# Ten slots instead of eight for the activation channel tiles of the in-projections

## The chip, the cores and the metric

The kernel runs on one core of one Trainium2 chip. The metric is the device time of one launch in microseconds, as the median of several runs. TensorE (PE) multiplies, VectorE (DVE), ScalarE (ACT) and GpSimd (POOL) do the elementwise work, and SyncE (SP) issues nearly all DMAs. Each engine, and SP's queue, works through its instructions in order: one that waits holds all behind it.

## The reference

One decoder layer of width 1024 on 2048 tokens, in float32. A normalized input goes through one combined projection, which feeds two groups of heads; both results meet in one output projection, and an MLP follows:

```python
u = rms_norm(h, norm_pre_mix[i])
q, k, v, qi, ki, wi, z, xbc, dt = jnp.split(u @ w_in[i], offsets, axis=-1)
ki = layer_norm(ki, k_idx_ln_w[i], k_idx_ln_b[i])
attn = sparse_attention(q, k, v, qi, ki, wi, rel_bias)   # each query keeps its best 256 keys
ssd = ssd_mixer(z, xbc, dt, ...)                         # convolution, chunked state scan, gate
h = h + rms_norm(jnp.concatenate([attn, ssd], -1) @ w_out[i], norm_post_mix[i])
f = jnp.square(jax.nn.relu(rms_norm(h, norm_pre_mlp[i]) @ w_mlp_up[i])) @ w_mlp_down[i]
h = h + rms_norm(f, norm_post_mlp[i])
```

The indexer's score of query t and key s is a sum over four small heads, `w[t,h] * relu(qi[t,h] . ki[s])`; the 256 largest scores of a query among the keys up to t take part in its softmax, with a bias by distance.

## The kernel before, in words

**Products.** A float32 operand is held as two parts, a rounded main part ("hi") and the rest ("lo"), and each product is three matmuls that add up in one PSUM bank: hi·hi (L257), hi·lo (L260), lo·hi (L261). Weights come by DMA into a raw tile (`load_w`, L246, tile `wr`) and are split by GpSimd into `wh` (L231) and `wl` (L232).

**The in-projections.** The tokens are cut into four tiles of 512. For each, `in_proj(t)` makes 20 products with the same eight activation channel tiles `u` (128 channels by 512 tokens, hi beside lo): first one of 76 columns with the weights `w_misc` (the index keys, the index weights and the time steps), then eight for the convolution inputs, two of index queries, four of gates, one of keys, one of values, and four of queries. Every product goes through the channels k = 0 to 7 in order, three matmuls each, 24 in all.

**The activation tiles.** `moving(t)` makes them. For each channel it takes a slot of the ring `u` and one of the ring `wr` (four slots, shared with all raw weights), loads the raw channel by DMA (`xr`, L301), writes hi on ScalarE (L311) and lo on VectorE (L312); for channels 3, 5 and 7 ScalarE scales the raw tile (L305) and copies hi (L308), and GpSimd makes lo (L309). `moving(t + 1)` stands at the last query product of tile t. Ring `u` has eight slots, so channel k of the next tile takes the slot of channel k of this one, and is written after that channel's last three matmuls. Below, the passage from the last product of a tile to the 76-column product of the next is called a change of tile; there are three.

**What runs beside them.** The main sequence is woven with other tasks by due times: the state scan of the SSM heads (`ssd`, with the tiles `si`, `cb`, `lm`, `xd`, the products `p_y`, `p_st`), the top-k search (`topk`: scores `p_ix` into rows `sc`, then counts by sign on ScalarE, `junk_k`, L610), and attention (`attention`: scores `p_s` from query stacks `qs`, bias rows `tq`, softmax rows `pp`, transposes `p_pt`, copies `ppt`, sums `p_o`, result `atp`). Queries pass through DRAM: ScalarE and GpSimd make `qp`, a DMA stores it to `q_d` (L393), and four small DMAs per block load `qs` (L570). Each task has a priority, and a scheduler of the framework puts all instructions of an engine into one order by its own model of times. The orders shown below are the result.

**Behind them.** The pool `front` is closed, and four windows follow, one per token tile: the output projection (`out_proj`: eight `mix` tiles, which take slots of the same ring `u`, L770; sums, and per block of tokens the residual `xh`, L801), and the MLP, whose activations (`u2`) take `u` slots too. Rest of the top-k and attention tasks is woven into the first three.

**Rings.** A tile is taken by `tl(tag, ...)` (L74 on), which asks `place(tag)` for a pool, a number of slots and a name. Where `rings` has an entry for the tag, `place` goes round that list; else the pool goes round its own slots.

Of the kernel before, what the change touches and what calls it, by code (L numbers as in the profile page):

```python
# [41 lines left out]
def hybrid_layer(ctx, tc, x, x_t, w_cols, n_post_mix, n_post_mlp, w_in, w_misc, dt_bias, a_log, d_skip,  # L42
# [11 lines left out]
    FC, BC = (2,3)  # L54
# [4 lines left out]
    WR = 4  # L59
    COMMON = dict(u=8, wr=WR, wl=WL, wh=WL, rsb=1, sc=2, mkk=1, qi=1, ks=2)  # L60
    ATT = dict(c2=2, qs=2)
    FRONT = dict(c4=FC, x24=1, m4=2, m2=3, kc=2, tq=1, mk=1)
    BACK = dict(c4=BC, x8=2, g4=9, m2=2)
    SSD = dict(si=3, cb=2, lm=1, xd=1)
    SIDE = [dict(kc=3, tq=1, mk=1), dict(kc=2, tq=1)]
# [1 line left out]
    where = {}  # L67
# [5 lines left out]
    rings = {}  # L73
# [12 lines left out]
    def phase(name, sizes, smalls=None, side="left"):  # L86
        stack = ExitStack()
        pool = stack.enter_context(tc.tile_pool(name=name, bufs=1, side=side, reuse_waits="tile"))
        use(pool, sizes)
        if smalls:  # L90
            use(pool, {smalls: 2})
        return stack
# [13 lines left out]
    def banks(name, sizes):  # L106
        stack = ExitStack()
        use(stack.enter_context(tc.tile_pool(name=name, bufs=1, space=PSUM, reuse_waits="tile")), sizes)
        return stack

    def const(ap, shape, name, dt=F32):
        t = cp.tile(shape, dt, name=name)
        SP.dma_start(t, ap)
        return t
# [6 lines left out]
    scan = phase("scan", SSD, "ssm", "right")  # L121
    front = phase("front", FRONT, "s")
    side_banks = banks("bank0", BANKS[0])
    NF = 4
    where["row"] = max(1024, 2 * NF * P)
    cols = const(w_cols, [P, 62], "cols")
    ident = const(c_ident, [P, P], "ident")
    junk_k = cp.tile([P, L], I8, name="junk_k")
# [805 lines left out]
    def weave(main, tasks):  # L934

        left = [[*e, 0] for e in tasks]
        now = 0.0
        while True:
            w = step("m", main)
            if w is None:  # L940
                break
            now += w
            for e in left:
                kind, g, n, a, b, done = e
                want = n * min(max((now - a) / (b - a), 0.0), 1.0)
                while e[5] < want:
                    e[5] += 1
                    step(kind, g)
                if now >= b and done <= n:
                    e[5] = n + 1  # L950
                    for _ in g:
                        pass
        for e in left:
            for _ in e[1]:
                pass

    def chain(*gens):
        for g in gens:
            yield from g
# [27 lines left out]
        tasks.append(ctask(range(4, NF), *PF))  # L987
    weave(chain(*(in_proj(t) for t in range(NT))), tasks)
    front.close()
    state["win"] = "1"  # L990
    back = ctx.enter_context(phase("back", BACK, "s"))
    MB = 4
# [95 lines left out]
```

## Time and profile before

| | |
|---|---|
| runs | 2916.97, 2921.40, 2927.34 us, median 2921.4 |
| the profiled execution | 2928.29 us |
| its span | 2926.5 us |
| TensorE busy | 2761.9 us, 94% of the span |
| GpSimd, VectorE, ScalarE busy | 60%, 56%, 51% |
| DMA | 383.46 MB, 131 GB/s on average |
| mean granted clock of TensorE | 0.973 of full |

The profile is that of one execution. A row of a timeline gives the start in us, the duration, the engine and line, the operation, the tile written and those read, the count, and, in brackets, how long the engine idled before it and what ended that. In the table by stretches a pair such as 19.99 (x107) is busy time and instructions of an engine, PEclk is the granted clock as a share of full speed, and the DMA share is the mean busy share of the sixteen DMA engines. The durations of matmuls overlap, since they are pipelined; the starts tell the pace.

### The profile page before, as it was taken

The numbers are of one execution on the slowest core, as the hardware profiler recorded it, in microseconds if no ns is written. First come the engines' busy times: TensorE is split into PE (matmuls) and PEld (weight loads), VectorE is DVE, ScalarE is ACT, GpSimd is POOL, SyncE is SP. The second block draws the span as 40 slices with busy tenths as digits, with TensorE's granted clock in tenths as the row PEclk, the third lists the DMA queues.
The fourth block names the chain that finished last, engine by engine and source line by source line (L and its number), as shares of the span: only waits on it lengthen the run. The fifth ranks groups of instructions, "written<-read, shape, count | busy, mean of one in ns | idle before, by whom it ended". The sixth has DMA issues, their size and how long they took to land.

```text
span 2926.5 us, 41201 instructions
## 1 busy us (share of the span) xinstructions
PE 2761.9 (94%) x13558; PEld 2250.7 (77%) x13558; DVE 1642.4 (56%) x4106; ACT 1481.5 (51%) x2550; POOL 1762.6 (60%) x1721
## 2 busy tenths in 40 slices
PE   7988989789989999998999999999999999999998
PEld 5766767667768887887787888878888888778886
DVE  5479588888575666747765565666444342511113
ACT  2375477675837575677773847644332332311101
POOL 4666556667666656654456575644564656588775
PEclk8999989999989999999999999999999999999999
DMA  3765654634733333255223222553222225522222
GB/s 128 224 189 151 218 157 149 208 118 160 249 120 119 112 103 102 90 176 180 101 94 98 90 97 79 170 177 102 87 95 81 93 78 177 204 95 97 95 94 86
DMA packets 286741, 383.46 MB, mean 131 GB/s; under 512 B 26520, under 2 KB 151360, under 8 KB 286528
## 3 DMA queue, kind: packets, MB, share of 16 engines
q1 hardware_dynamic: 286528, 380.84, 40.0%
q8 instruction: 107, 1.75, 0.2%
q14 instruction: 106, 0.87, 0.1%
HBM read 316.44 MB, written 64.30 MB: 130 GB/s over the span
## 4 chain that ended last, share of the span: by engine, by line
PE 67%; DVE 13%; ACT 6%; DMA 5%; issue 4%; POOL 3%; SPq 1%; POOLq 0%; DVEq 0%; ACTq 0%
PE p_mm L257 9%; PE p_mm L261 9%; PE p_mm L260 9%; PE p_dn L260 7%; PE p_dn L261 7%; PE p_dn L257 7%; ACT junk_k L610 5%; PE p_o L725 4%; PE p_s L683 4%; PE p_pt L717 3%; POOL wl L232 2%; PE p_ix L591 1%; DVE cnd L618 1%; PE p_acc L260 1%; PE p_acc L257 1%
## 5 line engine op out<-in xcount | busy, mean ns | idle before, releaser
L232 POOL TENSOR_TENSOR wl<-wr,wh 128x512 fp32r<-128x512 f32 (+1 forms) x740 | 987.0, 1335 | 179.6 <-ACT wh L229 107.0
L231 POOL TENSOR_SCALAR wh<-wr 128x512 fp32r<-128x512 f32 x674 | 449.6, 667 | 752.1 <-PE p_mm L260 372.8
L257 PE MATMUL p_mm<-u,wh 128*128 128x512 f32 (+1 forms) x1696 | 685.4, 404 | 47.4 <-ACT u L311 15.4
L261 PE MATMUL p_mm<-u,wl 128*128 128x512 f32 (+1 forms) x1696 | 682.8, 404 | 13.2 <-POOL wl L232 12.9
L260 PE MATMUL p_mm<-u,wh 128*128 128x512 f32 (+1 forms) x1696 | 674.9, 398 | 0.6 <-POOL u L309 0.3
L610 ACT ACTIVATE junk_k<-sc,cnd 128x512 int8<-128x512 f32 (+10 forms) x434 | 576.4, 1328 | 157.8 <-DVE cnd L618 122.2
L257 PEld LDWEIGHTS p_mm<-u,wh 128*128 128x128 f32 (+1 forms) x1696 | 322.9, 190 | 119.3 <-ACT u L311 17.5
L260 PE MATMUL p_dn<-wl,g 128*128 128x512 f32 x1008 | 402.2, 399 | 4.2 <-POOL wl L232 4.2
L261 PE MATMUL p_dn<-wh,g 128*128 128x512 f32 x1008 | 399.5, 397 | 2.7 <-POOL g L836 2.7
L261 PEld LDWEIGHTS p_mm<-u,wl 128*128 128x128 f32 (+1 forms) x1696 | 322.5, 190 | 88.7 <-POOL wl L232 21.3
L260 PEld LDWEIGHTS p_mm<-u,wh 128*128 128x128 f32 (+1 forms) x1696 | 322.6, 190 | 69.6 <-DVE u L312 2.3
L257 PE MATMUL p_dn<-wh,g 128*128 128x512 f32 x1008 | 328.0, 398 | 1.9 <-POOL wh L231 1.3
L834 ACT ACTIVATE r<-r 128x512 f32<-128x512 f32 x128 | 80.4, 629 | 437.1 <-DVE r L833 436.7
L688 DVE CUSTOM_DVE_ANT_0 pp<-p_s,mk 128x512 f32<-128x512 f32 (+3 forms) x320 | 192.5, 607 | 134.3 <-PE p_s L683 130.5
L719 ACT ACTIVATE ppt<-p_pt 128x512 fp32r<-128x512 f32 (+1 forms) x288 | 155.3, 568 | 208.1 <-PE p_pt L717 170.0
L720 DVE TENSOR_TENSOR ppt<-p_pt,ppt 128x512 fp32r<-128x512 f32 (+1 forms) x288 | 182.6, 655 | 129.6 <-ACT ppt L719 126.9
L260 PEld LDWEIGHTS p_dn<-wl,g 128*128 128x128 f32 x1008 | 190.3, 189 | 46.8 <-POOL wl L232 5.5
L261 PEld LDWEIGHTS p_dn<-wh,g 128*128 128x128 f32 x1008 | 190.3, 189 | 43.8 <-POOL g L836 3.1
L257 PEld LDWEIGHTS p_dn<-wh,g 128*128 128x128 f32 x1008 | 185.8, 189 | 42.0 <-POOL wh L231 2.9
L725 PE MATMUL p_o<-ppt,VV 128*128 128x256 f32 x1088 | 211.1, 294 | 1.9 <-DVE ppt L720 1.0
L617 DVE TENSOR_SCALAR keep<-cnt 128x1 int32<-128x1 f32 (+1 forms) x341 | 70.2, 206 | 244.1 <-ACT junk_k L610 242.7
L836 POOL TENSOR_TENSOR g<-r,g 128x512 fp32r<-128x512 f32 x128 | 170.1, 1331 | 53.2 <-ACT g L835 51.9
(253 smaller groups left out, 4177.6 us busy)
## 6 DMA issues: line engine op xcount, KB each, us to landing
wr<-w_up SPq DMA_DIRECT2D x256, 256.0 KB, 2.6
wr<-w_down SPq DMA_DIRECT2D x256, 256.0 KB, 2.6
wr<-w_in SPq DMA_DIRECT2D x160, 256.0 KB, 2.9
tq<-toep_d SPq DMA_DIRECT2D x128, 128.0 KB, 2.6
qs<-q_d SPq DMA_DIRECT2D x256, 64.0 KB, 2.5
wr<-w_out SPq DMA_DIRECT2D x64, 256.0 KB, 3.7
mix<-mix_d SPq DMA_DIRECT2D x32, 512.0 KB, 8.1
q_d<-qp SPq DMA_DIRECT2D x24, 512.0 KB, 3.6
```

Of the source, the lines that this page charges most:

```text
L231: G.tensor_scalar(dst_hi, src_f, 1.0, 0.0, op0=OP.mult, op1=OP.add)
L232: G.tensor_tensor(dst_lo, src_f, dst_hi.bitcast(F32), op=OP.subtract)
L257: m = PE.matmul(o, ah, bh, start=first, stop=False)
L260: PE.matmul(o, ah, bl, start=False, stop=False)
L261: state["mm3"] = PE.matmul(o, al, bh, start=False, stop=last).ins.name
L610: S.activation(junk_k[:, 0:n], scs[j], AF.Sign, bias=bias(j), accum_out=cnt[:, j:j + 1])
L683: PE.matmul(p[:, 0:w], qs[:, var, hh, :], K1[:, g, j0:j0 + w], start=var == 0, stop=var == 1)
L688: V.tensor_tensor_reduce(out=pp[:, j0:j0 + w], in0=p[:, 0:w], in1=mk[:, j0:j0 + w], scale=1.0, scalar=-3e38, op0=OP.add, op1=OP.max, accum ...
L719: S.activation(pg[:, 0, 0:w], p[:, 0:w], AF.Copy)
L720: V.tensor_tensor(pg[:, 1, 0:w], p[:, 0:w], pg[:, 0, 0:w].bitcast(F32), op=OP.subtract)
L725: PE.matmul(po[:, c0:c0 + 256], VV[:, kk, g, :], pg[:, part, j * 256:(j + 1) * 256], start=kk == 0 and part == 0, stop=kk == nb - 1 and pa ...
L836: G.tensor_tensor(gt[:, 1, :], r, gt[:, 0, :].bitcast(F32), op=OP.subtract)
```

## The change

While the in-projections run, the ring `u` has ten places: the eight of before and two more, tag `ux`, in the pool of the front phase (8 KB per partition together). After that phase the entry is taken out again, and `u` has its eight slots as before.

```diff
-    FRONT = dict(c4=FC, x24=1, m4=2, m2=3, kc=2, tq=1, mk=1)
+    FRONT = dict(c4=FC, x24=1, m4=2, m2=3, kc=2, tq=1, mk=1, ux=2)
...
     where["row"] = max(1024, 2 * NF * P)
+    rings["u"] = [where["u"]] * 8 + [where["ux"]] * 2
     cols = const(w_cols, [P, 62], "cols")
...
     front.close()
+    del rings["u"]
     state["win"] = "1"
```

The 32 channel tiles go round like this: tile 0 takes slots 0 to 7; tile 1 the two new ones, then 0 to 5; tile 2 takes 6 and 7 (unused since tile 0), the two new ones, then 0 to 3; tile 3 takes 4 to 7, the two new ones, then 0 and 1. The next two takers, the first two `mix` tiles of window 0, take slots 2 and 3, which are unused since tile 2. Their two DMAs move from the end of the in-projections to the third change of tile, where they follow a load of `w_in` weights.

Counts of instructions are the same on every engine. What differs is the order, from the first change of tile on. (The line numbers of the new kernel are higher by one from L126, and by two behind the end of the in-projections.) In the first change, on ScalarE, the hi copy of channel 0 moves ahead of a sign count and of a `qp` copy; on SP the DMA of raw channel 4 moves ahead of one `qs` and one `tq` load. In the third, on ScalarE, the hi copies of channels 0 and 1 move ahead of a `qp` copy. The second changes most; its raw channels 4 to 7 are `xr_4119`, `xr_4124`, `xr_4130` and `xr_4135`, and the first half of the next `w_misc` is `wr_4268`. On SP there, the order before:

```order
L301 DMA xr_4119<-x_t 128x512
L393 DMA q_d_92<-qp_3931 128x2x512
L301 DMA xr_4124<-x_t 128x512
L301 DMA xr_4130<-x_t 128x512
L676 DMA tq_3569<-toep_d_83 128x256
L486 DMA cb_4309<-cs_d1_3716 128x512
L570 DMA qs_3859<-q_d_92 64x2x128 x4
L676 DMA tq_3600<-toep_d_83 128x256
L393 DMA q_d_92<-qp_4093 128x2x512
L301 DMA xr_4135<-x_t 128x512
L246 DMA wr_4268<-w_misc 128x304
```

The order now:

```order
L677 DMA tq_3600<-toep_d_83 128x256
L571 DMA qs_3859<-q_d_92 64x2x128
L302 DMA xr_4119<-x_t 128x512
L302 DMA xr_4124<-x_t 128x512
L394 DMA q_d_92<-qp_3931 128x2x512
L302 DMA xr_4130<-x_t 128x512
L487 DMA cb_4309<-cs_d1_3716 128x512
L677 DMA tq_3755<-toep_d_83 128x256
L756 DMA mix_d_93<-atp_3415 128x4x128
L302 DMA xr_4135<-x_t 128x512
L756 DMA mix_d_93<-atp_3415 128x4x128
L247 DMA wr_4268<-w_misc 128x304
```

The loads of `tq_3569`, `qs_3859` and `tq_3600` stood between raw channel 4 and `w_misc`, and now stand ahead of raw channel 4; the load of another bias row, `tq_3755`, and two stores of an attention result stand there instead.

On ScalarE at the same place (`u_4097` and `u_4102` are channels 0 and 1 of the next tile, `lm_3721` and `cb_3720` belong to the state scan), before:

```order
L489 ACTIVATE lm_3721<-lm_3721,adt_3705 128x128 x4
L610 ACTIVATE junk_k_79,cnt_3277<-sc_3192,tiny_81 128x768
L490 ACTIVATE cb_3720<-cb_3720 128x512
L719 ACTIVATE ppt_3333<-p_pt_3328 128x512
L719 ACTIVATE ppt_3397<-p_pt_3394 128x256
L391 ACTIVATE qp_3931<-qf_3929 128x512
L311 ACTIVATE u_4097<-xr_4098,cols_75 128x512
L311 ACTIVATE u_4102<-xr_4103,cols_75 128x512
```

And now:

```order
L392 ACTIVATE qp_3825<-qf_3823 128x512
L611 ACTIVATE junk_k_79,cnt_3277<-sc_3192,cnd_3279 128x768
L737 ACTIVATE ot_3326<-p_o_3146 128x256
L312 ACTIVATE u_4097<-xr_4098,cols_75 128x512
L611 ACTIVATE junk_k_79,cnt_3277<-sc_3192,cnd_3279 128x768
L699 ACT_TABLE_LOAD
L699 ACTIVATE pp_3498,den_3492<-pp_3498,nm_3507 128x512
L490 ACTIVATE lm_3721<-lm_3721,adt_3705 128x128 x4
L491 ACTIVATE cb_3720<-cb_3720 128x512
L611 ACTIVATE junk_k_79,cnt_3277<-sc_3192,cnd_3279 128x768
L312 ACTIVATE u_4102<-xr_4103,cols_75 128x512
```

Channel 0's copy stood behind `lm_3721` and `cb_3720` and now stands ahead of them; so do a load of ScalarE's function table and a softmax row.

On TensorE, the end of the last product of the second tile, `p_mm_4066` (its channels 4 to 7 are `u_1589`, `u_1594`, `u_1600`, `u_1605`), before:

```order
L261 MATMUL p_mm_4066<-u_1600,wl_4062 128x512
L257 MATMUL p_mm_4066<-u_1605,wh_4061 128x512
L514 MATMUL p_y_3829<-lm_3721,xd_3737 64x128
L517 MATMUL p_st_3838<-xd_3737 128x256
L260 MATMUL p_mm_4066<-u_1605,wh_4061 128x512
L261 MATMUL p_mm_4066<-u_1605,wl_4062 128x512
L725 MATMUL p_o_3146<-ppt_3333,VV_86 128x256
L750 MATMUL p_at_3410<-ident_77,at_3136 128x128 x2
```

And the middle of it now:

```order
L261 MATMUL p_mm_4066<-u_1589,wh_4061 128x512
L718 MATMUL p_pt_3581<-ident_77,pp_3498 128x128
L751 MATMUL p_at_3410<-ident_77,at_3136 128x128 x2
L516 MATMUL p_y_3829<-cb_3720,st_90 64x128
L515 MATMUL p_y_3829<-lm_3721,xd_3737 64x128
L516 MATMUL p_y_3829<-cb_3720,st_90 64x128
L515 MATMUL p_y_3829<-lm_3721,xd_3737 64x128
L684 MATMUL p_s_3603<-K1_84,qs_3594 128x512 x2
L516 MATMUL p_y_3829<-cb_3720,st_90 64x128
L515 MATMUL p_y_3829<-lm_3721,xd_3737 64x128
L516 MATMUL p_y_3829<-cb_3720,st_90 64x128
L262 MATMUL p_mm_4066<-u_1589,wl_4062 128x512
```

The `cb` half of `p_y`, and matmuls of three attention steps, stood behind the product; they now stand in it, ahead of the third matmul of channel 4, with ten of its 24 matmuls behind them.

Behind the in-projections the differences are small rearrangements. The largest is on VectorE at the end of the second window's output projection: between its last sum and its first `xh` stand seven score sums (L596, five of them 512 wide and two 256), two first sums (L593), a softmax piece and a copy's rest, where two score sums, two copy's rests, a softmax piece and one first sum stood before.

## Rows read from the trace of the kernel before

**Rows 1.** The page: span, and busy time, share and instructions of each engine.
```profile
span 2926.5 us, 41201 instructions
...
PE 2761.9 (94%) x13558; PEld 2250.7 (77%) x13558; DVE 1642.4 (56%) x4106; ACT 1481.5 (51%) x2550; POOL 1762.6 (60%) x1721
```

**Rows 2.** Table by stretches: length, then the engines, clock, DMA share, rate.
```profile
core 0: us, PE busy (x) PEld busy (x) DVE busy (x) ACT busy (x) POOL busy (x), PEclk, DMA share, GB/s
161.00:190.00 29.00, 19.99 (x107) 14.50 (x106) 19.78 (x66) 24.56 (x69) 18.98 (x21) 0.76 0.66 208
350.00:369.00 19.00, 18.39 (x95) 15.03 (x93) 7.80 (x20) 6.16 (x16) 10.33 (x11) 1.00 0.70 219
369.00:402.00 33.00, 22.93 (x126) 16.76 (x124) 25.12 (x60) 28.07 (x64) 18.95 (x20) 0.74 0.59 186
570.60:600.00 29.40, 20.37 (x109) 15.01 (x110) 21.36 (x50) 26.02 (x53) 22.12 (x24) 0.83 0.52 166
760.00:780.00 20.00, 18.94 (x97) 15.03 (x97) 11.76 (x42) 17.58 (x34) 10.98 (x12) 1.00 1.02 382
800.00:860.00 60.00, 48.23 (x251) 38.98 (x250) 49.96 (x131) 27.28 (x62) 31.53 (x30) 0.86 0.39 130
```

**Rows 3.** TensorE's timeline at the three changes of tile.
```profile
160.72 0.39 PE L261 MATMUL p_mm<-u,wl 128*128 128x512 f32 x1
...
180.29 0.77 PE L257 MATMUL p_mm<-u,wh 128*76 128x512 f32 x1
...
368.69 0.40 PE L261 MATMUL p_mm<-u,wl 128*128 128x512 f32 x1
...
370.69 0.32 PE L515 MATMUL p_y<-cb,st 128*64 128x128 f32 x1
...
387.32 0.71 PE L257 MATMUL p_mm<-u,wh 128*76 128x512 f32 x1 [3.05 <-POOL wh L231]
...
570.21 0.39 PE L261 MATMUL p_mm<-u,wl 128*128 128x512 f32 x1
...
583.68 0.88 PE L514 MATMUL p_y<-lm,xd 128*64 128x128 f32 x4 [4.76 <-DVE lm L503]
...
586.43 0.99 PE L257 MATMUL p_mm<-u,wh 128*76 128x512 f32 x1
```

**Rows 4.** SP's queue in the first change.
```profile
168.99 2.53 SPq L570 DMA_DIRECT2D qs<-q_d  x4
...
176.64 3.48 SPq L570 DMA_DIRECT2D qs<-q_d  x4
...
181.32 0.38 SPq L246 DMA_DIRECT2D wr<-w_misc  x1
```

**Rows 5.** SP's queue in the second change.
```profile
365.47 6.21 SPq L301 DMA_DIRECT2D xr<-x_t  x3
...
375.26 2.53 SPq L570 DMA_DIRECT2D qs<-q_d  x4
379.48 0.33 SPq L676 DMA_DIRECT2D tq<-toep_d  x1
...
380.84 0.86 SPq L246 DMA_DIRECT2D wr<-w_misc  x1
```

**Rows 6.** ScalarE's timeline in the first change: channels 0 and 1.
```profile
164.10 1.32 ACT L311 ACTIVATE u<-xr,cols 128x512 fp32r<-128x512 f32 x2
```

**Rows 7.** ScalarE's timeline before the second change.
```profile
365.23 1.28 ACT L489 ACTIVATE lm<-lm,adt 128x128 f32<-128x128 f32 x4 [6.29 <-DVE lm L487]
```

**Rows 8.** ScalarE's timeline in the third change: channels 0 and 1.
```profile
569.25 0.71 ACT L311 ACTIVATE u<-xr,cols 128x512 fp32r<-128x512 f32 x1
...
572.97 0.71 ACT L311 ACTIVATE u<-xr,cols 128x512 fp32r<-128x512 f32 x1
```

**Rows 9.** The page, DMA issues: count, size of each, median us to landing.
```profile
mix<-mix_d SPq DMA_DIRECT2D x32, 512.0 KB, 8.1
```

**Rows 10.** VectorE's timeline at the end of the second output projection.
```profile
1392.85 0.75 DVE L596 SCALAR_TENSOR_TENSOR sc<-p_ix,wsc,sc 128x512 f32<-128x512 f32 x1
```

**Rows 11.** TensorE's timeline at the same place.
```profile
1399.59 0.33 PE L806 MATMUL p_tr<-ident,xh 128*128 128x128 f32 x1 [1.04 <-DVE xh L801]
```

## The prediction, made before the change was run

> **What bounds the kernel now.** The first view to read is the busy line of the page. TensorE is busy 2761.9 of 2926.5 us and every other engine stays at or below 60% [rows 1], so the whole kernel can win no more than TensorE's idle time, 164.6 us, and the time that its lower clock costs. The profiled execution took 2928.3 us, of which 1.8 lie around the span; the median of the runs shown, 2921.4, is 6.9 below it. I sum against 2928.3 and take the same difference from the median.
>
> The second view is the table by stretches [rows 2]. The ring of activation tiles can make something wait at three places only, the changes from one token tile to the next. TensorE idles 29.0 − 20.0 = 9.0 us in the first, 33.0 − 22.9 = 10.1 in the second and 29.4 − 20.4 = 9.0 in the third: 28.1 us. The other 136.5 us have other causes; the stretch from 800 to 860 alone, after the in-projections, holds 11.8.
>
> The third view is TensorE's timeline [rows 3]: where the last product of one tile ends, and where the 76-column product that opens the next begins. That is 161.11 to 180.29, 369.09 to 387.32 and 570.60 to 586.43, gaps of 19.2, 18.2 and 15.8 us, 53.2 in all, against 28.1 idle. So about half of the gaps is filled with the other tasks' matmuls, and an earlier first product is worth only the idle part of what it is earlier.
>
> The fourth view is the SP queue [rows 4, 5], since the opening product waits for a chain that ends there: raw channels, then the two halves of w_misc, then Pool's split of it. In the second change that last wait is 3.05 us for Pool's wh [rows 3].
>
> **The change, part by part.**
>
> *The work.* Nothing is added or removed: the same products, copies, DMAs and bytes. The price is in order and in waits.
>
> *Two more slots.* Before, channel k of the next tile may be written when the last product has used channel k of this one, so all sixteen copies of a change follow that product. Now channels 0 and 1 have slots that are free long before. A bound on what that can remove is the two of eight channels' share of the gaps, 53.2 × 2/8 = 13.3 us; below, each change is replayed by its own queue.
>
> *First change.* The SP queue is held by round trips of the attention task: four qs loads that end at 171.52, four more that end at 180.12, and only then, at 181.32, the second half of w_misc [rows 4]. These loads, and the q_d stores that they wait for, keep their places, and only channel 0's hi copy leaves the stretch on ScalarE: 1.32/2 = 0.7 us [rows 6]. I take −0.7, bounds 0 and −9.0, the idle time.
>
> *Second change.* Here the queue itself changes. Between raw channel 4, sent at some 371.3 (the third of the group at 365.47), and w_misc's first half at 380.84 stand four qs loads and a tq load that waits until 379.48 [rows 5]. From the first qs, 375.26, to the end of that tq, 379.81, this is 4.6 us. In the new order these five issues precede raw channel 4, at a time in which the queue waits anyway: the group of three raw channels holds it for 6.21 us. ScalarE has room to make their data early, with 6.16 of 19.0 us busy before the change [rows 2] and 6.29 us idle before the lm exponentials [rows 7]. So w_misc goes out 4.6 us earlier, and the opening product with it: −4.6. The idle time of 10.1 has room for that. Bounds: −10.1, and +5.1 for the halt that the second rival prices.
>
> *Third change.* Channels 0 and 1 have their hi copies ahead of the q copy before the product's end, so 0.71 + 0.71 = 1.4 us of ScalarE's work leave a stretch in which it is busy 26.0 of 29.4 us [rows 2, 8]. But TensorE waits there 4.76 us for the state task's lm [rows 3], which still follows most of the channel copies. I take −1.4, bounds 0 and −9.0.
>
> *Two mix loads.* Two of the first window's eight loads now find a free slot in the third change and stand there in the queue. Near 760 the DMA engines were full, 20 us at share 1.02 and 382 GB/s with TensorE idle for 1.1 [rows 2]. Two loads of 512 KB [rows 9] are 1.05 MB, by that rate 2.7 us. In the third change the share is 0.52, which leaves 14 us of free room, so I cost them at nothing; bounds +2.7 if they stand in front of w_misc's bytes, −1.1 if their absence frees the later stretch. The rule that speaks against this edit is in the Trainium skill, DMA: Bandwidth & Descriptors, section "Issuing engines are not separate DMA queues": all transfers run on the same 16 engines and interleave. By it the 2.7 us would fall on the weight loads of the change; the share of 0.52 [rows 2] makes that unlikely, and the sum goes without it.
>
> *The rest of the order.* The scheduler has re-sorted pieces up to the last windows. One place I can price: at the end of the second window's out-projection, before the first xh of VectorE, stand five more 512-wide score sums, 5 × 0.75 = 3.8 us at most, and TensorE waits for that xh, 1.04 us the first time [rows 10, 11]. Pieces like it go both ways elsewhere. I take 0 and bound the whole by one bad stretch, ±11.8 (800 to 860).
>
> **Sum.** −0.7 − 4.6 − 1.4 + 0 = −6.7 us: 2921.6 for a profiled execution like this one, 2914.7 for the median.
>
> **The clock.** In the changes TensorE's granted clock is 0.76, 0.74 and 0.83 of full, against 1.00 just before the second [rows 2]: part of the work runs at 1.2 instead of 2.4 GHz, after the engine idled. If all of it ran at full clock, 20.0 × 0.24 + 22.9 × 0.26 + 20.4 × 0.17 = 14.2 us would come back. I take nothing of it, since the gaps stay longer than 13 us. The Trainium skill, TensorE: Matmul & The Clock Gate, section "HAM oscillation — how this bites in real kernels", says that a wait that is long enough drops the clock and that the next work then starts cold; the rows agree, and by the rule a shortened wait could pay twice. That is the upper half of the first rival.
>
> **Rivals.**
>
> *The share rule (0.22).* If the rest of the chain moves up with its first two links, all three gaps shrink by a quarter: −13.3, 2908; with a quarter of the clock's cost, 3.6, 2904.5, and with all of it 2894. For it: ScalarE is nearly idle before the second change. Against it: only one or two copies in fact move in the first and third, and the chain passes SP's queue, not the slots alone.
>
> *The last product is halted (0.25, the other side).* In the new order four tasks' matmuls, among them the cb half of p_y, stand inside the last product of the second tile, with 10 of its 24 matmuls behind them. Before, that cb half ran at 370.69, 1.6 us after the product's end [rows 3]. On ScalarE its lm and cb now stand behind channel 0's copy, a table load and a softmax row. If they become ready no earlier, TensorE, in order, holds the product until 370.69; then follow 1 to 2 us of p_y (eight of its matmuls are left, and four take 0.88 [rows 3]) and 10 matmuls at 18.39/95 = 0.19: an end at 373.6 to 374.6 instead of 369.09, 5.1 late, with all later channels behind it. The sum is −0.7 + 5.1 − 1.4 = +3.0, 2924.4, and with the 3.8 us of the hand-over 2928.2. It decides as soon as the halt is over 2.1 us, what the other two changes give. Against it: the 6.29 us of idle time before lm [rows 7] hide 3 us of other copies easily, if their inputs are there.
>
> *Nothing (0.17).* SP's round trips and ScalarE's load are the bound, and the early copies only wait: 2921.4. The first change speaks for this, the second against it.
>
> *The forecast (0.36):* 2914.7, own range 2909 to 2919.
>
> **How the numbers follow.** 0.3%, about what a measurement of this kernel tells from no change, is 8.8 us: faster is below 2912.6, slower above 2930.2. Faster: 0.40 of the forecast, 0.85 of the share rule, 0.15 of nothing, 0.04 of the halt: 0.37. Slower: 0.07, 0.02, 0.20 and 0.50 of them (the unpriced re-order of ±11.8 included): 0.19. Same: 0.44. The range goes from 2897, near the share rule with the clock given back, to 2931, the halt with the hand-over and some of the re-order.
>
> **What would show it.** Right: in the second change w_misc's first half goes out at about 376 and the opening product begins near 383, TensorE's idle time there about 5 us; the first change's gap is unchanged within 1 us, the third's shorter by about 1.4; the mix loads lie in the third change, with the weight loads' landings as before. Wrong: a wait of over 2 us inside the last product of the second tile; a gap in the first change that shrinks by more than 3 us; a difference larger than 5 us that arises after 760, where no slot is missing.

## The result, and the profile after

The change makes the kernel slower: 2939.28 us median (2938.39 to 2944.05, 4 runs) against 2921.96 (2916.97 to 2927.34, 4 runs); the ratio is 1.0064, with a 95% interval of 1.0046 to 1.0081. The forecast was 2914.7, with a range from 2897 to 2931. The profiled execution took 2938.39 us.

The page of the changed kernel, span and busy line as in [rows 1]:

```profile
span 2936.6 us, 41227 instructions
...
PE 2772.9 (94%) x13558; PEld 2260.6 (77%) x13558; DVE 1653.7 (56%) x4106; ACT 1482.7 (50%) x2550; POOL 1770.0 (60%) x1721
```

The two spans differ by 2936.6 − 2926.5 = 10.1 us, less than the medians: the profiled execution of the kernel before was 6.9 us above the median that the prediction took, and in that of the changed kernel the first tile ran 5.2 us faster, though both issue the same there, as shown below.

TensorE idles 2936.6 − 2772.9 = 163.7 us, against 164.6 before: the idle time has not grown. It is busy 11.0 us longer with the same 13,558 instructions. Most of that fits the clock. By the clock records of the two traces, TensorE was busy at 1.2 GHz, half its clock, for 133.7 us, against 116.7 before. The matmuls of a product start 0.43 us apart at this level (629.9 us of the changed kernel's trace) and 0.23 at the full one (559.2 us), so the 17.0 us more at half clock make some 8 us more busy time (an estimate).

TensorE's timeline of the changed kernel at the three changes of tile, to set beside [rows 3] (its line numbers are one higher):

```profile
155.57 0.39 PE L262 MATMUL p_mm<-u,wl 128*128 128x512 f32 x1
...
172.51 0.71 PE L258 MATMUL p_mm<-u,wh 128*76 128x512 f32 x1 [0.26 <-POOL wh L232]
...
364.68 0.38 PE L516 MATMUL p_y<-cb,st 128*64 128x128 f32 x2
...
367.90 0.40 PE L262 MATMUL p_mm<-u,wl 128*128 128x512 f32 x1
...
377.94 0.71 PE L258 MATMUL p_mm<-u,wh 128*76 128x512 f32 x1 [0.78 <-POOL wh L232]
...
559.43 0.39 PE L262 MATMUL p_mm<-u,wl 128*128 128x512 f32 x1
...
575.44 0.70 PE L515 MATMUL p_y<-lm,xd 128*64 128x128 f32 x4 [6.29 <-DVE lm L504]
...
578.06 0.99 PE L258 MATMUL p_mm<-u,wh 128*76 128x512 f32 x1
```

The gaps from the last product of a tile to the one that opens the next were 19.2, 18.2 and 15.8 us and are 16.6, 9.6 and 18.2. The second has halved, as its queue said. The third has grown: the matmul that waits for the state scan's lm now waits 6.29 us instead of 4.76. The `p_y` rows inside the second tile's last product stand there without a bracket, and TensorE is busy 14.11 of the 14.30 us up to the product's end: nothing is halted.

SP's queue of the changed kernel in the second change, to set beside [rows 5]:

```profile
358.49 1.88 SPq L571 DMA_DIRECT2D qs<-q_d  x3
...
362.50 0.57 SPq L571 DMA_DIRECT2D qs<-q_d  x1
...
370.84 0.40 SPq L247 DMA_DIRECT2D wr<-w_misc  x1
```

The query loads have passed before the product's end, and w_misc goes out 370.84 − 368.30 = 2.5 us after it, against 380.84 − 369.09 = 11.8 before.

So the changes of tile are 8.8 us shorter in all, and the kernel is 17 us slower. Where that goes is read from stretches between the same two products. One is the last tile, from the start of its sixth product to that of its eleventh (the 76-column product is the first of the 21 of a tile). Others lie in the windows. The table by stretches, of the kernel before:

```profile
634.80:671.50 36.70, 34.98 (x174) 28.03 (x175) 28.97 (x73) 28.15 (x53) 22.62 (x25) 0.95 0.37 109
842.10:1021.60 179.50, 177.70 (x879) 147.31 (x880) 108.43 (x304) 106.88 (x188) 121.03 (x118) 1.00 0.35 111
1411.50:1733.10 321.60, 313.90 (x1572) 261.65 (x1573) 192.07 (x467) 214.47 (x300) 200.44 (x186) 0.98 0.29 94
1995.40:2495.30 499.90, 498.93 (x2619) 420.68 (x2618) 200.88 (x481) 159.22 (x249) 285.28 (x287) 1.00 0.31 102
```

and of the changed kernel, with the second change as its first row:

```profile
368.30:394.00 25.70, 20.42 (x116) 15.45 (x115) 18.00 (x48) 22.10 (x53) 17.82 (x19) 0.87 0.67 204
...
628.90:674.70 45.80, 40.59 (x195) 31.56 (x196) 33.73 (x89) 30.62 (x57) 25.19 (x29) 0.87 0.29 92
842.40:1031.00 188.60, 183.84 (x918) 153.07 (x919) 122.33 (x323) 117.89 (x203) 121.61 (x118) 0.99 0.34 107
1420.20:1748.00 327.80, 315.92 (x1557) 263.31 (x1557) 192.03 (x452) 211.03 (x295) 200.99 (x187) 0.97 0.28 90
2012.50:2505.80 493.30, 489.17 (x2526) 410.98 (x2525) 187.44 (x449) 150.04 (x234) 285.17 (x287) 1.00 0.31 101
```

The same five products take 45.8 instead of 36.7 us. TensorE does 21 more matmuls of other tasks in it, idles 5.2 instead of 1.7 us, and has a clock of 0.87 instead of 0.95. The 21 matmuls are work that is done here instead of elsewhere, so not all of the 9.1 us is a loss. In the second change itself the clock is better, 0.87 against 0.74 [rows 2]. The first two stretches of the windows take 9.1 and 6.2 us more than before; the third, with 93 matmuls fewer, gives 6.6 back, and the step from the in-projections to the first MLP product gives 3.7. There is no single place.

A caution for all such comparisons. Up to the last product of the first tile both kernels issue the same matmuls in the same order, the other engines too have one order up to 154.5 us of the trace of before, and yet the two executions differ there by 5.2 us. Before:

```profile
0.00:154.30 154.30, 132.78 (x534) 99.86 (x535) 81.70 (x177) 54.48 (x94) 84.78 (x93) 0.94 0.55 177
```

and changed:

```profile
0.00:149.10 149.10, 129.79 (x534) 98.49 (x535) 79.19 (x177) 54.98 (x95) 85.00 (x93) 1.00 0.56 183
```

534 matmuls each, at a clock of 0.94 and of 1.00. In the 19 traces of this document that begin with these matmuls, the last of them starts at 148.9 to 154.6 us. Behind this first tile the order repeats better. Two runs below (ten slots in the old order, and the mix loads moved) have the old order on TensorE again; there the five products take 37.9 and 37.4 us:

```profile
632.00:669.90 37.90, 36.05 (x175) 28.57 (x176) 29.66 (x73) 28.27 (x53) 22.70 (x25) 0.93 0.37 105
633.50:670.90 37.40, 35.68 (x174) 28.39 (x175) 29.27 (x73) 28.22 (x53) 22.66 (x25) 0.94 0.36 107
```

No product of these two traces starts more than 4.4 us off that of before. Differences of that size between single traces show nothing; verdicts below go by the runs.

### The profile page after: what moved, and what is told of

Read it like the earlier page. It is cut to its first block, busy times and chain, and to the rows that moved or that the text cites. A ratio compares the mean times of both kernels' runs of the same rounds, so it can differ in the third digit from the quotient of the medians.

```text
span 2936.6 us, 41227 instructions
## 1 busy us (share of the span) xinstructions
PE 2772.9 (94%) x13558; PEld 2260.6 (77%) x13558; DVE 1653.7 (56%) x4106; ACT 1482.7 (50%) x2550; POOL 1770.0 (60%) x1721
## 3 DMA queue, kind: packets, MB, share of 16 engines
q1 hardware_dynamic: 286528, 380.84, 39.8%
## 4 chain that ended last, share of the span: by engine, by line
PE 63%; DVE 8%; ACT 3%; POOL 3%; issue 2%; DMA 2%; POOLq 0%; DVEq 0%; ACTq 0%; SPq 0%
PE p_mm L262 8%; PE p_mm L258 8%; PE p_mm L261 8%; PE p_dn L261 7%; PE p_dn L262 7%; PE p_dn L258 7%; PE p_o L726 4%; PE p_s L684 4%; PE p_pt L718 3%; ACT junk_k L611 2%; POOL wl L233 1%; PE p_acc L258 1%; PE p_acc L261 1%; PE p_acc L262 1%; PE p_ix L592 1%
## 5 line engine op out<-in xcount | busy, mean ns | idle before, releaser
L699 ACT ACTIVATE pp<-pp,nm 128x128 f32<-128x128 f32 (+15 forms) x128 | 153.3, 1198 | 112.4 <-DVE nm L696 93.4
```

Source lines behind the costliest of these rows:

```text
L699: S.activation(pp, pp, AF.Exp, bias=nm, accum_out=den[:, h:h + 1])
```

## The experiments

The change does two things: it gives ten slots, and it makes the scheduler sort all that follows anew. To separate them, a kernel with the slots of the changed one is given an order: behind the build of the layer, each instruction gets an edge to the one that shall precede it on its engine. Such an edge fixes the order of issue and asks for no wait. The lists are those of the kernel before ("old") and of the changed one ("new"), or one up to a time of its trace and the other for what is left. Where nothing else is said, a kernel below is the changed one with such lists, and only the lists differ.

```diff
+def issue_order(nc, tc):
...
+            if last is not None:
+                tc.add_manual_dep(i, last, keep, reason="issue order")
+            last = i.name
...
         hybrid_layer(tc, *args)
+        issue_order(nc, tc)
```

### Slots or order

Ten slots, old order everywhere. 

> The ring has ten slots, and every engine and SP's queue issue their instructions in the order of the kernel before, instruction by instruction. Theory R (the loss of 17 us comes from the re-sorted order alone; the slots cost nothing): 2918 to 2925 us, as before, since the old order does not use the two early slots. Theory S (the slots themselves cost: other addresses, early raw loads, waits of the mix tiles): 2935 to 2942 us.

Measured: 0.9998 of the kernel before (0.9986 to 1.0010). The slots and their place in memory cost nothing, and in an order that does not use them they win nothing. Of theory S the early transfers are left, which the old order does not start early; the next run starts those of two changes of tile early and is faster, and the two mix loads by themselves cost nothing (further below). So theory S falls.

New order up to 415 us, old behind. 

> Ten slots; the new order for all that the changed kernel issued before 415 us of its trace (two changes of tile), and the order of before for the rest. Theory R: the second change keeps what it won (10.6 us shorter in the trace), the first tile's stretch behind the first change keeps what it lost (5.1 us), nothing later is lost: -3 to -8 us, 2914 to 2919. Theory S: slower than before by more than 8 us, 2930 or more. If the gain of the second change is only work put off to later, the time is that of before, 2921 within 2.

Measured: 0.9980 (0.9971 to 0.9989), 2917.7 us. Theory R's number. Its median and ratio are the lowest of all runs, and it beats both kernels, the one before by 0.1 to 0.3%.

Old order up to 545 us, new behind. 

> Ten slots; the order of before for all that the kernel before issued before 545 us of its trace (two changes of tile), and the new order for the rest: the third change, the last tile and the windows. Theory R: these lose 15 to 22 us in the comparison of the traces, so 2936 to 2943. If the loss of the changed kernel has its root before 545 us and only shows later: 2919 to 2926.

Measured: 1.0097 (1.0079 to 1.0114), 2949.7 us. The loss lies behind 545 us, and is here even larger than expected. In the same five products of the last tile, this kernel's trace has the row of the changed one again:

```profile
645.10:690.50 45.40, 40.44 (x195) 31.39 (x196) 33.17 (x89) 30.87 (x59) 25.48 (x29) 0.87 0.29 93
```

Twelve slots, in the scheduler's own order:

```diff
-    FRONT = dict(c4=FC, x24=1, m4=2, m2=3, kc=2, tq=1, mk=1, ux=2)
+    FRONT = dict(c4=FC, x24=1, m4=2, m2=3, kc=2, tq=1, mk=1, ux=4)
...
-    rings["u"] = [where["u"]] * 8 + [where["ux"]] * 2
+    rings["u"] = [where["u"]] * 8 + [where["ux"]] * 4
```

> Twelve slots (four more), in the order that the scheduler makes of it. If the order is a lottery with no trend (theory R): any time from 2905 to 2945. If more slots cost more by themselves (theory S): 2945 to 2960. If more early channels give more: the second change as short as with ten, and all in all below 2935.

Measured: 1.0090 (1.0075 to 1.0105). By itself this fits S (2945 to 2960 us), and at 2949.8 us it lies above the range of R; the runs above have already decided against S, so R's range was too low.

### Which stretch

The second change of tile alone (old to 345, new to 415, old). 

> Ten slots; the order of before up to 345 us of its trace, then the new order up to 415 us of the changed kernel's trace (the second change of tile alone), then the order of before again. Theory R (the second change wins what its queue order wins, 10.6 us in the comparison of the traces, and the stretch of the first change loses 5.1): -8 to -11 us, 2913 to 2916. If the gain of the second change needs the new order ahead of it, as its idle ScalarE was made there: between 2918 and 2924.

Measured: 0.9984 (0.9973 to 0.9995), that is −4.7 us of 2924.66. That is less than the 10.6 us of the trace, and at 2919.9 us it lies in the range of the second theory, that the gain needs the new order ahead of it; but with that order ahead (the run up to 415 us) it is −5.8, and the two intervals overlap. It is just what the sum had for this step, −4.6, and the two times that the prediction named, 376 and 383, stand in its trace:

```profile
376.47 0.70 SPq L247 DMA_DIRECT2D wr<-w_misc  x1
...
383.32 0.71 PE L258 MATMUL p_mm<-u,wh 128*76 128x512 f32 x1 [1.53 <-POOL wh L232]
```

The gap is only 7.7 us here: of the 40 matmuls of other tasks that stood in it 16 are left, and the product ahead of it holds 28 instead of 11. That product ends at 375.6 us instead of 369.1, a part of which arises earlier, near the join. A shorter gap is not a gain of the same size.

New order for all in-projections, old for the windows. 

> Ten slots; the new order for all in-projections (up to 746 us of the changed kernel's trace), the order of before for the windows. By the drift between the two traces, from the first tile's end (-5.2) to the first window (+1.0), the in-projections lose 6.2 us of the 17: 2927 to 2933. If the whole loss lies in the in-projections, 2938 or more; if it lies in the windows alone, 2915 to 2922.

Measured: 1.0034 (1.0020 to 1.0048), +9.9 us of 2924.66, just above what was expected. With −5.8 up to 415 us, the rest of the in-projections loses 15.7. The five products have the same row a third time:

```profile
637.80:683.30 45.50, 40.51 (x195) 31.55 (x196) 33.27 (x89) 30.64 (x57) 25.28 (x29) 0.87 0.29 93
```

Old order for the in-projections, new for the windows. 

> Ten slots; the order of before for all in-projections, the new order for the windows. By the same drift the windows lose 9 to 11 us: 2932 to 2936. If the windows' order costs nothing by itself and only carries on what came before: 2921 to 2926.

Measured: 1.0053 (1.0036 to 1.0071), 2937.6 us, somewhat more than expected. So both halves lose. Together they would make 0.87%, and the full new order loses 0.64, which the intervals alone would allow. But a join of two orders seems to cost something of its own: in this kernel's trace the stretch from the last in-projections to the first MLP product, where the join is, takes 7.1 us longer than before; in the changed kernel, without a join, it is 3.7 shorter.

New order from 545 to 646 us. 

> Ten slots; the order of before but for the third change of tile and the first half of the last tile (545 to 646 us), which have the new one, the two mix loads in the third change among it. By the drift this stretch loses 8 us, with the state scan's matmuls on TensorE waiting for lm (11.4 us of waits in the last tile against 4.8): 2929 to 2935. If the loss of the last tile comes from what is behind it: 2921 to 2926.

Measured: 1.0059 (1.0045 to 1.0072), 2941.2 us, six more than the upper end.

New order for the third change alone, 545 to 592 us. 

> Ten slots; the order of before but for the third change of tile alone (545 to 592 us), on all engines and the queue. If the loss of the longer stretch (17 us) lies in the change of tile itself, as 6.3 us of wait for lm there and the clock behind it suggest: 2930 to 2942. If it lies in the products behind the change: 2920 to 2927.

Measured: 1.0040 (1.0024 to 1.0056). Both lose, but each has two joins, and in both traces the stretch at the first join, ahead of the third change, is already 6 us longer than before; the changed kernel has it 0.8 shorter. How much of these two losses is the stretch's and how much the join's is not settled.

### Inside the third change

The queue alone, and the engines alone (TensorE, VectorE and ScalarE; GpSimd keeps the old order), have the new order from 545 to 646 us. 

> Ten slots and the order of before, but on SP's queue the stretch from 545 to 646 us (third change, first half of the last tile) has the new order: w_misc ahead of a q_d round trip and the two mix loads in the third change. The engines keep their old order. Theory Q (the mix loads and the queue's order cost the 17 us that this stretch's whole new order cost): 2933 to 2941. Theory E (the engines' order costs it): 2919 to 2927.

> The same stretch the other way round: TensorE, VectorE and ScalarE have the new order from 545 to 646 us, SP's queue and GpSimd the old one. Theory E: 2933 to 2943, with TensorE waiting for the state scan's lm. Theory Q: 2919 to 2927.

Measured: 1.0048 (1.0032 to 1.0064) and 1.0052 (1.0038 to 1.0065). Each half alone loses as much as both together, so both theories got their number and neither is shown. The waits of SP's queue in the first of them tell why such a split says little (who waits, for whom, us in total, times, longest):

```profile
SPq L571 <- PE p_ix L592: 11.3, 1, 11.3
SPq L302 <- DVE ends L494: 6.7, 1, 6.7
```

The loads of `qi`, which the new order has ten places further ahead, wait 11.3 us for a matmul that TensorE's old order has late, and the raw channels behind them wait too: the gap of the third change is 27.8 us in this trace. So the mixing of two orders has a loss of its own.

Only the two mix loads moved to the third change, all else in the old order (two entries of SP's list). 

> Ten slots and the order of before on every engine and the queue, but the first window's first two mix loads (1.05 MB) stand in the third change of tile behind the first w_in load, as in the changed kernel. The prediction priced this move at nothing, with bounds +2.7 and -1.1 us. If it holds: 2921 to 2927 beside 2924 for before. If the loads in front of the weights are a main cause of the loss: 2930 or more, with Pool or TensorE waiting for w_in weights at 590 to 605 us.

Measured: 0.9990 (0.9980 to 0.9999). The move costs nothing, as priced: −2.9 us by the ratio, with an interval from −5.8 to −0.3.

Next, the waits for the state scan. The waits of TensorE in the last tile, of the kernel before (563 to 744 us):

```profile
PE p_y L514 <- DVE lm L503: 4.8, 1, 4.8
```

and of the changed one (554 to 746):

```profile
PE p_y L515 <- DVE lm L504: 11.4, 4, 6.3
```

They suggest that the scan's matmuls stand too early in TensorE's order. In the first of these runs four groups of them were moved behind matmuls of products, in the changed kernel's order; in the second, one group in the fastest version; in the third, one group alone in the changed kernel's order. (Edits of TensorE's list alone.)

> The changed kernel's own order on every engine, but in the last tile four groups of the state scan's matmuls on TensorE, for which it waits 6.3, 2.9, 2.4 and 0.7 us in the trace, stand 10 to 19 matmuls of the waiting product later, so that the product runs while their inputs are made. Theory W (the loss in the last tile is TensorE held in order by these waits, and the half clock behind them): some 12 us of waits and 3 to 5 us of clock go, a part comes back as other waits: 2925 to 2933, against 2939. If VectorE is the bound there and the product waits instead: 2937 to 2942.

> The fastest version so far (new order to 415 us, old order behind it), with one such group of the third change moved behind 12 matmuls of the opening product, for which TensorE waits 4.1 us. Theory W: 2 to 5 us less than 2918, 2913 to 2916. If the product waits instead: 2917 to 2921.

> The changed kernel's own order, but one matmul group of the state scan (p_st), which stands between the second and the third matmul of a channel of a product in the last tile and holds TensorE 2.9 us for VectorE there, stands ten matmuls later, behind that product. If such a hold costs its wait and the half clock behind it: -3 to -5 us, 2934 to 2937 beside 2939 for the changed kernel. If the scan is what the rest waits for, as the four groups moved together suggest (they cost 15 us): 2939 to 2945.

Measured: 1.0108 (1.0092 to 1.0123), with a median 15 us above the changed kernel's instead of 6 to 14 below, outside both theories; 0.9987 (0.9979 to 0.9996), not faster than without the edit; and 1.0048 (1.0035 to 1.0062), with a median of 2939.5, which cannot be told from the changed kernel (1.0046 to 1.0081). Theory W falls. TensorE's timeline with the four groups moved, at the third change:

```profile
578.31 0.71 PE L258 MATMUL p_mm<-u,wh 128*76 128x512 f32 x1 [6.65 <-POOL wh L232]
```

The product ahead ends at 562.8 us, so the gap is 15.5 us instead of 18.2: the opening product does come earlier. But TensorE idles just as long, 6.65 instead of 6.29 us, now for GpSimd's split of w_misc, and from the opening product to the sixth it then takes 59.0 instead of 50.8 us. GpSimd's timeline there:

```profile
575.57 1.06 POOL L502 TENSOR_TENSOR xd<-xd,ends 128x256 f32<-128x256 f32 x1
576.59 1.26 POOL L505 TENSOR_TENSOR cb<-cb,si 128x512 f32<-128x512 f32 x1
577.82 0.44 POOL L232 TENSOR_SCALAR wh<-wr 128x304 fp32r<-128x304 f32 x1
```

GpSimd has the split in order behind two multiplications of the same scan. Its input was hardly earlier: the first half of w_misc goes out at 574.4 us, and the two halves land after 2.8 and 3.3 us. And what is moved back comes due further on, as in the run with one group moved:

```profile
656.86 0.88 PE L497 MATMUL p_x<-ident,si 128*128 128x128 f32 x3 [5.58 <-DMA si<-s_d]
```

There TensorE waits 5.58 us for the input of a next step of the scan, where the longest such wait in the changed kernel's last tile is 1.5, and the five products take 48.2 us. So taking out these waits did not help in any of the three runs; that the scan, GpSimd and the queue hold each other in balance is an argument, not shown.

### Orders without the slots

The kernel before with eight slots, with the start of the state scan's due times moved by 2 us either way:

```diff
-    SS = (90,170)
+    SS = (92,170)
```

> The kernel before with eight slots and one number changed that has nothing to do with slots: the state scan's due times begin 2 us later in the weaving (92 instead of 90). The scheduler re-sorts as many instructions as in the change under study (10,300 of 12,973 on TensorE stand elsewhere). Theory R as a lottery (a re-sort of this size costs or gains some 5 to 30 us by itself, whatever causes it): outside 2915 to 2932, more likely above. If it takes the slots to lose: 2917 to 2929.

The other way it is `SS = (88,170)`. 

> The kernel before with eight slots and the state scan's due times 2 us earlier in the weaving (88 instead of 90); 2,366 of 12,973 instructions on TensorE stand elsewhere. If a re-sort costs by itself whatever causes it: 2930 to 2950. If the first draw with eight slots was bad luck: 2915 to 2928.

And nine slots, as above with one slot in `ux`. 

> One extra slot, in the scheduler's own order (9,763 of 12,973 instructions on TensorE stand elsewhere than before, as many as with two). If the re-sort sets the time and not the slots: 2930 to 2950, as with ten and twelve and with the re-sort of eight. If the loss grows with the slots (0.6% with two, 0.9% with four): near 2933.

Measured: 1.0077 (1.0061 to 1.0092), 1.0072 (1.0059 to 1.0085) and 1.0106 (1.0093 to 1.0120). The page of the first:

```profile
span 2946.0 us, 41235 instructions
...
PE 2771.5 (94%) x13558; PEld 2254.9 (77%) x13558; DVE 1649.8 (56%) x4106; ACT 1478.7 (50%) x2550; POOL 1768.9 (60%) x1721
```

and of nine slots:

```profile
span 2953.8 us, 41223 instructions
...
PE 2777.6 (94%) x13558; PEld 2261.7 (77%) x13558; DVE 1646.7 (56%) x4106; ACT 1478.3 (50%) x2550; POOL 1765.1 (60%) x1721
```

Five re-sorts, with eight, eight, nine, ten and twelve slots, lose 0.77, 0.72, 1.06, 0.64 and 0.90%. There is no trend with the slots, and a change that has nothing to do with them loses as much. Nine slots lie even above the range expected. So the order of the kernel before is better than five of five others that this scheduler made; why it is, and whether others would be as good, is not shown.

Nor do the changes of tile tell which order is good. With eight slots and the scan 2 us earlier the three gaps are 14.3, 12.8 and 11.1 us (the opening products begin at 178.3, 387.9 and 591.6 us), 15 us less than before in all, and the kernel loses 0.72%. What the five traces have in common is more busy time on TensorE, by 7 to 16 us, and more of it at half clock, 129 to 146 us against 116.7 before and 116.8 and 112.5 in the two runs with the old order. Its idle time is as before in the changed kernel and 7 to 12 us longer in the other four.

## Why the prediction was wrong

**The step that failed** is "the rest of the order. I take 0 and bound the whole by one bad stretch, ±11.8". It should have been the largest term. The new order behind 545 us loses 28 us where it stands alone (1.0097), 8 of them at the join in its trace; in the changed kernel's own trace, without a join, what follows the start of the last product ahead of the third change takes 19.7 us longer. By runs, the in-projections behind 415 us lose 15.7 us and the windows alone 15.5 (1.0053). "Pieces like it go both ways elsewhere" had no row behind it: of five re-sorts none won. The bound was one stretch of the kernel, while 9,973 of 12,973 instructions on TensorE had changed their place.

**What bounds the kernel.** "It can win no more than TensorE's idle time and the time that its lower clock costs" was right as a limit for gains, but the loss was looked for in waits alone. In the changed kernel TensorE's idle time is as before, and its busy time 11.0 us longer, some 8 of them at half clock: in the last tile the clock over five products was 0.87 of full instead of 0.95. The section on the clock took only what a shorter wait could give back; that the new order could cost clock elsewhere was left out.

**First change:** −0.7 forecast. The gap is 2.6 us shorter, but the products behind it are 5.1 us slower in the changed kernel's trace. By runs, the new order up to 415 us wins 5.8 us and the second change alone 4.7, so the first change and the products behind it make −1.1, which the intervals do not tell from 0.

**Second change:** −4.6 forecast, −4.7 measured alone (interval −1.5 to −7.9). The mechanism was right: the five issues passed before the product's end, w_misc went out at 376.5 and the opening product began at 383.3 us, about as named, and in the changed kernel TensorE idles 5.3 us there, where about 5 were named. That the numbers agree so closely is in part luck: the interval is wide, the product ahead ends 6.5 us later than the forecast had it, and the matmuls that move from the gap into that product were not in the sum. With them, the gap of the changed kernel is 8.6 us shorter, and w_misc goes out 9.2 us earlier after the product's end, both more than was won.

**Third change:** −1.4 forecast, and the gap is 2.4 us longer; alone the stretch costs 11.7 us (1.0040), of which its trace shows 6 at the join. The step read a wait for lm as the only one. Close behind it, before the change too, stands GpSimd's split of w_misc, which waited for the transfer:

```profile
584.94 0.45 POOL L231 TENSOR_SCALAR wh<-wr 128x304 fp32r<-128x304 f32 x1 [1.14 <-DMA wr<-w_misc]
```

The bracket of a row in [rows 3] names one releaser, not what ends shortly after it.

**Mix loads:** 0 forecast with bounds +2.7 and −1.1; measured 0.9990 alone. At a DMA share of 0.52 in that stretch the room was enough for 1.05 MB more.

**The hand-over in the second window:** 3.8 us were priced as a risk, and it did not come. From the last sum of that output projection to the first MLP product it is 27.9 us instead of 28.8, and TensorE idles 7.6 instead of 10.1 us in it. The output projection ahead of it is 4.5 us longer.

**The rivals.** The halt did not happen: the `cb` half of `p_y` runs inside the product with no wait. That rival had the right side by luck, with the wrong mechanism. The share rule gave −13.3 for the gaps; they shrank by 8.8, to no avail. "Nothing" was refuted by the second change. What came true, that a new order loses by itself in many places, was not among the four; with it the range would have had to reach 2950.

**How it was wrong by its own tests:** "a difference larger than 5 us that arises after 760" was named as a sign, and it came: the windows' new order alone loses 15.5 us. The other two signs, a wait inside the last product of the second tile and a first gap more than 3 us shorter, did not.

## What to carry to other kernels

Where a scheduler orders the program, a change of resources is two changes: what the resource allows, and a new order of all that follows. The second cannot be priced from the stretches that one can replay, nor by how many instructions move: with 1,018 of the 12,973 places on TensorE changed (up to 415 us) the kernel won 0.20%, with 125 (the third change alone) it lost 0.40, with 8,077 (the windows) 0.53. Here five of five re-sorts of a good order lost 0.6 to 1.1%, so give that a chance and a size of its own. To use the first without the second, hold the old order by edges and let only the place that profits have the new one: here this turned +0.64% into −0.20%.

Be wary of cutting an order by engine, or of moving one group because of a wait that the profile names. In the five runs that did so here nothing was won, and in the traces shown other waits came in its place. A shorter gap is no proof either; the two ends of the gap have to be looked at.

## What was not expected of the hardware

Two executions of the same 534 matmuls in the same order, from the start to 150 us, differed by 5.2 us, with granted clocks of 0.94 and 1.00. Over 19 traces the last of these matmuls starts at 148.9 to 154.6 us, with clocks of 0.92 to 1.00; at a clock of 0.94 alone it starts at 151.9 to 154.6. So the clock is not all of it, and what sets it in one execution is not shown.
